# Two-layer attention trunk in split fp32: later score slots, token-tile stores for the turned q, k and gate, and a different final norm and store

## The chip, the cores and the metric

The kernel runs on one core of a Trainium2 chip. The metric is device time in microseconds (us) from launch to end, the median of several runs. The engines are named as in the profile: PE is TensorE (PEld its weight loads), DVE is VectorE, ACT is ScalarE, POOL is GpSimd and SP is SyncE, which here only issues DMAs. A letter q behind an engine's name (SPq, POOLq) stands for what it issues.

## The reference, cut to what matters

256 tokens of width 2048 go through two layers. Each layer is norm, one wide input projection, attention, a gate, one output projection and a residual add; a last norm closes.

```python
def _layer_c(x, norm_g, w_in, w_out, pos):
    h = jnp.matmul(_rmsnorm(x, norm_g).astype(x.dtype), w_in).astype(jnp.float32)
    cq, ck, cv, z = jnp.split(h, [C_WIDTH, 2 * C_WIDTH, 3 * C_WIDTH], axis=-1)
    yc = _moba_attention(_rope(_heads(cq, C_HEADS), pos), _rope(_heads(ck, C_HEADS), pos), _heads(cv, C_HEADS))
    y = _merge(yc) * jax.nn.silu(z)
    return x + jnp.matmul(y.astype(x.dtype), w_out)

def reference(x, ...):
    h = x
    for i in range(DEPTH):
        ...
    return _rmsnorm(h, final_norm).astype(x.dtype)
```

Layer 1 has 16 heads of 128; with 256 tokens its block attention is plain causal attention. Layer 0 has the same shape with two kinds of heads: eight heads whose three dilated windows are combined by their softmax denominators (which is one softmax with a count mask), and four differential heads (a softmax minus a learned multiple of a second one, times a value of width 256, then a norm).

## The kernel before, in words

**The projections.** Each layer is a row of 20 chunks of 512 output columns: four groups g of q, k, z (the gate) and v (g = 0 runs v, q, k, z), then four chunks `o` of the output projection. A chunk has 16 slots, one for each 128 rows of the contraction. In a slot PE runs `mm3` for each of two token tiles (128 tokens): three matmuls (high times high, high times low, low times high) give fp32 accuracy out of two rounded parts. So a slot is six matmuls of 512 columns, and the program has 40 chunks. The weights arrive as `raw` tiles of 1 MB (four slots, three buffers, issued by SP, L96) and are split for two slots at a time: ACT writes the high part `wh` (L122), then DVE the low part `wl` (L123). Split m serves slots 2m and 2m + 1 of the whole program. There are four buffers for each part, so ACT can write `wh` m only when PE is done with split m - 4.

**Between the projections.** `at(slot, f, ...)` puts a function behind the matmuls of a slot, and the loop over chunks calls what is due. For a finished q or k chunk, `nxt` is the first slot after it:

- `evac_rope` (L262) scales and rotates one token tile on DVE (L270 to L273, tiles `rt`), and `turn` (L233) transposes blocks of 32 by 32 within it (L235, tile `bz`). Tile 0 is due at `nxt`, tile 1 at `nxt + 2`.
- `place` (L238) follows tile 1: POOL stores both turned tiles to DRAM in one DMA of 512 KB (L243, tensor `dt`) and loads them back with eight DMAs of 64 KB (L247, four for each token tile), which finishes the transpose.
- `split_rope` (L278), at `nxt + 13`, splits the loaded tile into `kh`, `kl` (or `qh`, `ql`) on ACT and DVE (L285, L286), a token tile at a time for k.
- `attn_s` or `diff_s`, from `nxt + 14`, do the scores `ps_s` (L317 reads the raw tile `k`, then `mm3` the split ones) and the softmax. `attn_t` sends the probabilities `p` through DRAM in the same way (L356, L360), `attn_h` splits them (L369), and `attn_o` or `diff_o` with `diff_y` multiply by v and gate with the turned z (tile `u`).

These slots are due times. A scheduler puts each engine's instructions into one fixed list, and may draw something forward or push it back by where it thinks the data will be. Each engine then works through its list in order and waits at the first instruction whose input is missing. `order` rows below are taken from these lists.

**The end.** `last_chunk` (L456) runs token tile 0 as one piece of 512 columns and token tile 1 as two of 256. After each piece DVE adds the residual (L484), ACT squares and sums (L486), DVE adds to the mean (L491), POOL raises it to the power -0.5 (L493), DVE and ACT scale four pieces of 512 columns (L499, L501), and SP stores each (L502). At the start PE runs `WARM` matmuls on a constant (L137) before the first weights are split.

## Time and profile before

| | |
|---|---|
| median of 3 runs | 1003.44 us (997.42 to 1008.15) |
| the profiled execution, its time | 999.49 us |
| its span, first to last instruction | 997.7 us |
| mean granted TensorE clock | 0.971 |
| PE busy | 942.4 us (94%) |
| DVE busy | 643.0 us (64%) |
| ACT busy | 474.5 us (48%) |
| POOL busy | 200.5 us (20%) |
| HBM read and written | 192.23 MB and 20.19 MB, 213 GB/s over the span |

A busy PE is PE with a matmul in flight; at a lower granted clock the same matmul is busy for longer, so that busy time alone does not tell of a loss there. The rows in the prediction come from four kinds of views: the page (busy shares, costliest groups), the list of who waited for whom (engine, operation, line, what it waited for: us in total, times, longest), the timeline (start, duration, engine, line, operation, with the idle time before it and what ended that in brackets) and a table by stretches (length, busy time of each engine with the number of instructions, granted clock, DMA share, GB/s).

### The profile page before, as it was taken

To read this page: it belongs to the slowest core of one execution; us is meant where nothing else is said; L and a number is where in the kernel's file an instruction comes from. 1 tells how busy PE (TensorE), PEld (TensorE's weight loads), DVE (VectorE), ACT (ScalarE), POOL (GpSimd) and SP (SyncE) were. 2 spreads that over 40 slices of the span, in tenths; PEclk is the share of its full clock that TensorE was granted. 3 is DMA by queue.
4 is the path that set the end of the run, shared out by engine and by line. 5 is a ranking of instruction groups with operands and counts; after the bars stand their busy time and mean duration, and the time that the engine had idled before them with its cause. 6 is when DMAs were issued, how large, how long until landed. Compare 5 with 4: busy or idle time off the path is not lost. (4 is left out here: it accounts for less than half of the span.)

```text
span 997.7 us, 11928 instructions
## 1 busy us (share of the span) xinstructions
PE 942.4 (94%) x4276; PEld 778.8 (78%) x4276; DVE 643.0 (64%) x999; ACT 474.5 (48%) x711; POOL 200.5 (20%) x368
## 2 busy tenths in 40 slices
PE   8999997999799988999999999979996999799996
PEld 7887886888688867888888878868885888587886
DVE  6666875756566666665555768747664766575572
ACT  7534643553355335554554454535442644264451
POOL 0021441321113110300000125215011421132000
PEclk9999999999989998999999999989997999899999
DMA  9786776566645664655555668667665756676542
GB/s 329 259 320 232 242 241 212 198 210 244 214 161 210 213 232 137 220 196 174 187 193 185 237 212 266 219 199 234 212 209 180 245 198 211 211 241 227 187 169 84
DMA packets 42827, 213.21 MB, mean 214 GB/s; under 512 B 9040, under 2 KB 9808, under 8 KB 22672
## 3 DMA queue, kind: packets, MB, share of 16 engines
q1 hardware_dynamic: 27504, 175.21, 50.1%
q0 software_dynamic: 14976, 36.20, 11.4%
q10 hardware_dynamic: 288, 1.05, 0.3%
q8 instruction: 33, 0.54, 0.2%
q14 instruction: 26, 0.21, 0.1%
HBM read 192.23 MB, written 20.19 MB: 213 GB/s over the span
## 5 line engine op out<-in xcount | busy, mean ns | idle before, releaser
L312 PE MATMUL acc<-wh,x 128*128 128x512 f32 x2048 | 655.1, 397 | 1.6 <-ACT wh L119 1.6
L123 DVE TENSOR_TENSOR wl<-raw,wh 128x1024 fp32r<-128x1024 f32 x314 | 382.7, 1220 | 206.1 <-ACT wh L122 205.3
L122 ACT ACTIVATE wh<-raw 128x1024 fp32r<-128x1024 f32 x314 | 332.0, 1059 | 359.8 <-PE acc L312 322.2
L312 PEld LDWEIGHTS acc<-wh,x 128*128 128x128 f32 x2048 | 390.7, 191 | 81.9 <-ACT wh L119 1.8
L312 PE MATMUL acc<-wl,x 128*128 128x512 f32 x1024 | 405.1, 396 | 0.2 <-DVE wl L120 0.2
L312 PEld LDWEIGHTS acc<-wl,x 128*128 128x128 f32 x1024 | 196.0, 191 | 39.8 <-DVE wl L120 0.5
L312 PE MATMUL acc<-wh,yh 128*128 128x512 f32 x224 | 88.3, 394 | 0.0
L312 PE MATMUL acc<-wl,yh 128*128 128x512 f32 x224 | 87.4, 390 | 0.0
L312 PE MATMUL acc<-wh,yl 128*128 128x512 f32 x224 | 87.3, 390 | 0.0
L243 POOL DMA_DIRECT2D dt<-bz x24 | 13.6, 568 | 305.6 <-DVE bz L235 302.1
L360 POOL DMA_DIRECT2D p<-d x112 | 61.2, 554 | 56.8 <-DMA d<-bt 29.5
L317 PE MATMUL ps_s<-k,q 128*128 128x128 f32 x64 | 14.7, 315 | 41.8 <-DMA k<-dt 41.6
L317 PEld LDWEIGHTS ps_s<-k,q 128*128 128x128 f32 x64 | 12.8, 214 | 47.0 <-issue 29.8
L312 PEld LDWEIGHTS acc<-wh,yl 128*128 128x128 f32 x224 | 42.0, 188 | 9.1 <-DVE yl L389 0.3
L312 PEld LDWEIGHTS acc<-wl,yh 128*128 128x128 f32 x224 | 42.1, 188 | 8.4
L312 PEld LDWEIGHTS acc<-wh,yh 128*128 128x128 f32 x224 | 42.1, 188 | 8.2
L247 POOL DMA_DIRECT2D q<-dt x64 | 34.7, 550 | 39.2 <-ACT wh L122 19.7
L247 POOL DMA_DIRECT2D k<-dt x64 | 34.7, 549 | 32.6 <-DMA dt<-bz 19.6
L356 POOL DMA_DIRECT2D d<-bt x28 | 15.7, 561 | 124.3 <-DVE st L328 85.6
L247 POOL DMA_DIRECT2D u<-dt x64 | 34.7, 549 | 19.0 <-DMA p<-d 13.2
L286 DVE TENSOR_TENSOR kl<-k,kh 128x512 fp32r<-128x512 f32 x16 | 11.0, 688 | 39.1 <-ACT kh L285 39.1
L285 ACT ACTIVATE kh<-k 128x512 fp32r<-128x512 f32 x16 | 10.0, 624 | 44.3 <-DMA k<-dt 44.2
(122 smaller groups left out, 663.8 us busy)
## 6 DMA issues: line engine op xcount, KB each, us to landing
raw<-in_w SPq DMA_DIRECT2D x124, 1024.0 KB, 5.2
raw<-in_o SPq DMA_DIRECT2D x32, 1024.0 KB, 4.8
dt<-bz POOLq DMA_DIRECT2D x24, 512.0 KB, 4.2
d<-bt POOLq DMA_DIRECT2D x28, 192.0 KB, 4.3
p<-d POOLq DMA_DIRECT2D x112, 48.0 KB, 4.7
q<-dt POOLq DMA_DIRECT2D x64, 64.0 KB, 3.6
k<-dt POOLq DMA_DIRECT2D x64, 64.0 KB, 6.2
u<-dt POOLq DMA_DIRECT2D x64, 64.0 KB, 4.6
```

Of the source, the lines that this page charges most:

```text
L122: nc.scalar.activation(ht, r, AF.Copy)
L123: nc.vector.tensor_sub(lt, r, ht.bitcast(F32))
L243: nc.gpsimd.dma_start(d, bt.rearrange("p c t h j -> p c (t h j)"))
L247: nc.gpsimd.dma_start(t[32 * c:32 * c + 32, tt].rearrange("p a h j -> p a (h j)"), dv[c, tt])
L285: nc.scalar.activation(a, v, AF.Copy)
L286: nc.vector.tensor_sub(b, v, a.bitcast(F32))
L312: nc.tensor.matmul(out_, l, r, start=start and i == 0, stop=stop and i == 2)
L317: nc.tensor.matmul(ps[:, 0:P], q[:, h * P:(h + 1) * P], k[:, 0, :, h], start=True, stop=True)
L356: nc.gpsimd.dma_start(d, bt.rearrange("p c b j -> p c (b j)"))
L360: nc.gpsimd.dma_start(pt[32 * c:32 * c + 32], dv[c])
```

## The change

- `turn` now does the whole way for one token tile: its own `bz` (two buffers) and its own `dt` (256 KB, four buffers), stored as soon as that tile is turned. After tile 1 the eight loads are written as before, those of tile 0 from the first tensor and those of tile 1 from the second. `place` is gone.
- Tile 1 is due at `nxt + 1` (was `nxt + 2`).
- `split_rope` is due at `nxt + 18` (was 13). The first scores are due at `nxt + 22`, in the last group of a layer (g = 3, `late`) at `nxt + 20` (was 14). The slots of `attn_t`, `attn_h`, `attn_o`, `diff_o`, `diff_y` follow; for the heads of `attn_s` the distance from the last `attn_t` to its `attn_h` stays at 12 slots, and is 10 in the last group.
- `last_chunk`: the sum of squares is one DVE instruction with an accumulator (`tensor_tensor_reduce`) that starts from the mean so far; the last 256 columns are scaled and multiplied by the norm's weights in one instruction; the pieces are 256 and 512 columns wide, DVE's are stored by SP and ACT's by ACT itself, and token tile 1 has six pieces (was four).
- `WARM` is 13 (was 10).

```diff
-WARM = 10
+WARM = 13
...
-    def turn(src, bt, tt):
-        nc.vector.transpose(bt[:, :, tt].rearrange("p c h j -> p h c j"),
-                            src.rearrange("p (h c j) -> p h c j", h=4, c=4))
-    def place(bt, name):
-        t = work.tile([P, 2, 4, 4, 32], F32, tag=name, name=name)
-        d = dram.tile([P, 4, S], F32, tag="dt", name="dt")
-        nc.gpsimd.dma_start(d, bt.rearrange("p c t h j -> p c (t h j)"))
-        dv = d.rearrange("(a i) c (t x) -> c t i a x", a=4, t=2)
-        for tt in range(2):
-            for c in range(4):
-                nc.gpsimd.dma_start(t[32 * c:32 * c + 32, tt].rearrange("p a h j -> p a (h j)"), dv[c, tt])
-        return t
+    def turn(src, box, name):
+        tt = len(box)
+        bt = work.tile([P, 4, 4, 32], F32, tag="bz", name="bz", bufs=2)
+        nc.vector.transpose(bt.rearrange("p c h j -> p h c j"), src.rearrange("p (h c j) -> p h c j", h=4, c=4))
+        d = dram.tile([P, 4, P], F32, tag="dt", name="dt", bufs=4)
+        nc.gpsimd.dma_start(d, bt.rearrange("p c h j -> p c (h j)"))
+        box[tt] = d.rearrange("(a i) c x -> c i a x", a=4)
+        if tt == 1:
+            box["t"] = t = work.tile([P, 2, 4, 4, 32], F32, tag=name, name=name)
+            for i in range(2):
+                for c in range(4):
+                    nc.gpsimd.dma_start(t[32 * c:32 * c + 32, i].rearrange("p a h j -> p a (h j)"), box[i][c])
...
-                nc.scalar.activation(j, x, AF.Square, accum_out=fs[:, tt, i:i + 1])
...
+                mean = e5[:, tt, 3 + i:4 + i]
+                nc.vector.tensor_tensor_reduce(out=j, in0=x, in1=x, scale=1.0 / D, scalar=part, op0=ALU.mult,
+                                               op1=ALU.add, accum_out=mean)
+                part = mean
+                if i + 1 == len(widths):
+                    nc.gpsimd.tensor_tensor(rf, mean, half, op=ALU.pow)
+                if tt == 0 or i == 0:
+                    nc.vector.tensor_mul(x, x, gf[1][:, CW + at_col:CW + at_col + w])
...
+            pieces = ((0, 256), (256, 768), (768, 1280), *last), ((1280, 1536), (1536, mid))
...
+                    (nc.sync, nc.scalar)[e].dma_start(out[tt * P:(tt + 1) * P, c[0]:c[1]], x)
...
-                    at(nxt + 2 * tt, evac_rope, ps, kind, (Q, K)[kind == "k"], layer, g, tt, box)
+                    at(nxt + tt, evac_rope, ps, kind, (Q, K)[kind == "k"], layer, g, tt, box)
             if kind != "z":
-                at(nxt + 13, split_rope, kind, (Q, K)[kind == "k"], layer, g, box)
+                at(nxt + 18, split_rope, kind, (Q, K)[kind == "k"], layer, g, box)
...
+            late = g == 3
+            first = nxt + (20 if late else 22)
...
-                    at(nxt + 14 + 3 * h, attn_s, layer, g, h, md if layer == 0 else mc, box)
-                    at(nxt + 17 + 3 * h, attn_t, box)
-                    at(nxt + 32 + 2 * h, attn_h, box)
-                    at(nxt + 34 + 2 * h, attn_o, layer, g, h, box)
+                    at(first + 3 * h, attn_s, layer, g, h, md if layer == 0 else mc, box)
+                    at(first + 3 + 3 * h, attn_t, box)
+                    at(first + (13 if late else 15) + 3 * h, attn_h, box)
+                    at(first + (15 if late else 17) + 3 * h, attn_o, layer, g, h, box)
```

The diff moves a few numbers; what they do to the lists stands in the following rows, all of the last group of layer 1. There k's chunk ends at slot 544 (`nxt`), `acc544` is the gate's chunk and `acc560` that of v, `x0` to `x15` are the 16 slots of a chunk, and split m serves slots 2m and 2m + 1, so that the number behind `wh` tells the slot. Line numbers of the change differ by a few from those of before (L243 is L242, L247 is L248, L285 is L279, L122 is L123).

PE, the place of the first score matmul of the group, before:

```order
L312 MATMUL acc544_6717<-wh279_6812,x14_115 128x512
L317 MATMUL ps_s_6880<-k_6761,q_6593 128x128
L312 MATMUL acc544_6717<-wh279_6812,x15_116 128x512
L312 MATMUL acc544_6717<-wl279_6813,x15_116 128x512
L312 MATMUL acc544_6717<-wh279_6812,x15_116 128x512 x2
```

and with the change:

```order
L306 MATMUL acc560_6952<-wh282_6934,x4_108 128x512
L311 MATMUL ps_s_7030<-k_6818,q_6652 128x128
L306 MATMUL ps_s_7030<-kh_7008,qh_6839 128x256
L306 MATMUL ps_s_7030<-kl_7009,qh_6839 128x256
L306 MATMUL ps_s_7030<-kh_7008,ql_6840 128x256
L306 MATMUL acc560_6952<-wh282_6934,x5_109 128x512
```

The first score moves from the gate's slot 15, which is `nxt` + 15, to v's slot 5, `nxt` + 21 (in the other groups to `nxt` + 23), and is now followed at once by its other three matmuls.

ACT, the place of the copies that split k, before:

```order
L122 ACTIVATE wh281_6846<-raw140_6798 128x1024
L122 ACTIVATE wh282_6868<-raw141_6832 128x1024
L285 ACTIVATE kh_6862<-k_6761 128x4x128
L122 ACTIVATE wh283_6901<-raw141_6832 128x1024
L285 ACTIVATE kh_6862<-k_6761 128x4x128
```

and with the change:

```order
L123 ACTIVATE wh279_6884<-raw139_6831 128x1024
L279 ACTIVATE kh_7008<-k_6818 128x4x128
L123 ACTIVATE wh280_6900<-raw140_6870 128x1024
L123 ACTIVATE wh281_6918<-raw140_6870 128x1024
L279 ACTIVATE kh_7008<-k_6818 128x4x128
L123 ACTIVATE wh282_6934<-raw141_6904 128x1024
```

Although `split_rope` is due five slots later, its copy of token tile 0 now stands three weight splits earlier, ahead of split 280 (needed at slot 560, `nxt` + 16), and that of tile 1 two earlier, ahead of split 282 (`nxt` + 20). All eight groups have this distance.

POOL, the store and the loads of k (`dt` and `k`) and what follows, before:

```order
L243 DMA dt_6762<-bz_6728 128x1024
L247 DMA k_6761<-dt_6762 32x4x128 x8
L356 DMA d_6926<-bt_6924 128x384
L243 DMA dt_6965<-bz_6911 128x1024
L360 DMA p_6886<-d_6926 32x4x96 x4
```

and with the change:

```order
L242 DMA dt_6800<-bz_6798 128x512
L248 DMA k_6818<-dt_6800 32x4x128 x4
L242 DMA dt_6816<-bz_6814 128x512
L248 DMA k_6818<-dt_6816 32x4x128 x4
L242 DMA dt_6970<-bz_6968 128x512
L248 DMA u_6987<-dt_6970 32x4x128
```

The four loads of tile 0 stand ahead of the store of tile 1, though the code writes them behind it; the store of tile 1 waits in this list until they are issued.

## The prediction

> **What bounds the kernel now.** I first read the page's busy shares and the list of waits. The columns of the latter are engine, operation, line, what it waited for, and the time in total, the number of waits and the longest.

> ```profile
> PE 942.4 (94%) x4276; PEld 778.8 (78%) x4276; DVE 643.0 (64%) x999; ACT 474.5 (48%) x711; POOL 200.5 (20%) x368
> PE ps_s L317 <- DMA k<-dt: 41.6, 7, 7.9
> PE ps_s L312 <- ACT kh L285: 1.8, 2, 1.6
> ```

> PE is the bound, and nearly all its idle time behind the start is one wait: the first score matmul of a group waits for the k that comes back from DRAM, seven times of eight, for 41.6 us. The timeline shows where, and how fast PE runs otherwise.

> ```profile
> 75.56 0.39 PE L312 MATMUL acc<-wl,x 128*128 128x512 f32 x1
> 76.24 0.39 PE L312 MATMUL acc<-wl,x 128*128 128x512 f32 x1
> ...
> 174.25 0.77 PE L317 MATMUL ps_s<-k,q 128*128 128x128 f32 x2 [5.91 <-DMA k<-dt]
> ...
> 868.92 0.76 PE L317 MATMUL ps_s<-k,q 128*128 128x128 f32 x2 [6.69 <-DMA k<-dt]
> ```

> From one `wl` matmul to the next there are 0.68 us and three matmuls, so a slot of six is 1.36 us. Two of the seven waits stand in brackets. Such a wait has a second price, seen when the stretch of 10 us that begins with its end is asked for. The columns are the stretch, its length, busy time of PE, PEld, DVE, ACT and POOL, granted clock, DMA share and GB/s.

> ```profile
> 96.95:106.95 10.00, 9.75 (x46) 7.92 (x47) 7.32 (x20) 7.96 (x17) 0.00 (x0) 1.00 0.50 175
> 174.25:184.25 10.00, 10.00 (x41) 8.29 (x42) 6.01 (x17) 6.59 (x16) 0.00 (x0) 0.80 0.33 113
> 274.88:284.88 10.00, 10.00 (x37) 8.25 (x38) 5.15 (x15) 5.46 (x13) 0.00 (x0) 0.71 0.30 106
> 378.05:388.05 10.00, 10.00 (x39) 8.28 (x40) 5.50 (x15) 5.97 (x13) 0.00 (x0) 0.75 0.31 107
> 664.34:674.34 10.00, 10.00 (x38) 8.26 (x39) 5.37 (x16) 5.94 (x13) 0.00 (x0) 0.73 0.32 114
> 767.36:777.36 10.00, 10.00 (x39) 8.29 (x40) 5.64 (x17) 6.23 (x14) 0.00 (x0) 0.76 0.30 105
> 868.92:878.92 10.00, 10.00 (x37) 8.26 (x38) 5.26 (x16) 6.01 (x12) 0.00 (x0) 0.72 0.30 105
> ```

> PE is busy all through, but at a mean clock of 0.71 to 0.80 after six of the waits: it lost 2.0 + 2.9 + 2.5 + 2.7 + 2.4 + 2.8 = 15.3 us of work. The seventh, the shortest, left the clock at 1.00. So the late k costs 41.6 + 15.3 = 56.9 us of the span of 997.7.

> **The change, part by part.** *Later scores.* The scores go from `nxt` + 15 to `nxt` + 23 (+ 21 in the last group of a layer), which is 8 x 1.36 = 10.9 us later (8.2). The longest wait was 7.9 us (in the list of waits), so on this count alone the 41.6 us and the clock loss go. What is late next? The copies that split k, since ACT's list now has them ahead of weight splits (the rows of the change). Their deadline, counted from the end of k's chunk: `wh` and `wl` of slot 16 are needed at 16 x 1.36 = 21.8 us, and kh, wh and wl come one after the other:

> ```profile
> L123 DVE TENSOR_TENSOR wl<-raw,wh 128x1024 fp32r<-128x1024 f32 x314 | 382.7, 1220 | 206.1 <-ACT wh L122 205.3
> L122 ACT ACTIVATE wh<-raw 128x1024 fp32r<-128x1024 f32 x314 | 332.0, 1059 | 359.8 <-PE acc L312 322.2
> L285 ACT ACTIVATE kh<-k 128x512 fp32r<-128x512 f32 x16 | 10.0, 624 | 44.3 <-DMA k<-dt 44.2
> ```

> 0.62 + 1.06 + 1.22 and 0.2 for the hand-overs are 3.1 us. So token tile 0 may land at 18.7 us, and tile 1 (slot 20, 27.2 us) at 24.1 us, before PE waits. Queued behind the waiting copy on ACT are the next `wh`, then the gate's evacuation; behind those `wl` on DVE, and PE behind both. How long k takes, from the second group of layer 0 (first q, then k, then the store, the loads and the landing) and from the first group, where it came quickest:

> ```profile
> 123.30 0.75 DVE L270 SCALAR_TENSOR_TENSOR rt<-acc,rn,cosN 128x512 f32<-128x512 f32 x1 [0.35 <-PE acc L312]
> 128.25 0.70 DVE L235 STREAM_TRANSPOSE bz<-rt 128x512 f32<-128x512 f32 x1
> 133.16 0.70 DVE L235 STREAM_TRANSPOSE bz<-rt 128x512 f32<-128x512 f32 x1
> 147.98 0.75 DVE L270 SCALAR_TENSOR_TENSOR rt<-acc,rn,cosN 128x512 f32<-128x512 f32 x1 [0.71 <-PE acc L312]
> 151.69 0.63 ACT L285 ACTIVATE qh<-q 128x512 fp32r<-128x512 f32 x1 [2.59 <-DMA q<-dt]
> 155.23 0.71 DVE L235 STREAM_TRANSPOSE bz<-rt 128x512 f32<-128x512 f32 x1
> 160.29 0.70 DVE L235 STREAM_TRANSPOSE bz<-rt 128x512 f32<-128x512 f32 x1
> 161.29 0.56 POOL L243 DMA_DIRECT2D dt<-bz  x1 [15.87 <-DVE bz L235]
> 165.39 4.33 POOL L247 DMA_DIRECT2D k<-dt  x8 [3.55 <-ACT wh L122]
> 174.04 0.63 ACT L285 ACTIVATE kh<-k 128x512 fp32r<-128x512 f32 x1 [5.96 <-DMA k<-dt]
> ...
> 91.57 4.34 POOL L247 DMA_DIRECT2D k<-dt  x8 [3.29 <-DMA dt<-bz]
> 96.67 0.63 ACT L285 ACTIVATE kh<-k 128x512 fp32r<-128x512 f32 x1 [1.72 <-DMA k<-dt]
> ```

> From the end of k's chunk (147.98) the turn of tile 0 starts at 7.25 us, since DVE stood behind q's split (151.69), while for q it starts at 4.95. Tile 1's starts at 12.31 (q: 9.86), the store at 13.31, the loads 4.10 later, and k is there 8.65 after the first load (5.10 in the first group), at 26.06.

> *Stores by token tile.* q gains the same way and lands before k's rotation, so I put the turn of k's tile 0 between the two rows, at 6.3, and its store at 7.3. The half store I give the whole one's 4.10: loads at 11.4. Four loads move half of what eight do, so I take a landing between 5.10 and 8.65, 6.5: tile 0 at 17.9, 0.8 us early. POOL issues four loads in 4.33 / 2 = 2.17 us and takes tile 1's store only then (13.6; its turn ends by about 12), so its loads start at 17.7 and land at 24.2, 0.1 late. With 5.10 nothing waits; with 8.65 tile 0 is 1.35 and tile 1 2.25 us late, 2.25 a group. I take 0.8 a group for the scatter, **6.5 us** for eight groups (0 to 18); no such wait is long enough for the clock. The 24 extra stores cost POOL 24 x 0.56 = 13.4 us at 20% busy, under PE's cover unless they delay loads, which the sum above counts.

> [...]

> *Scores' end.* The heads' p follow later, and the output projection does not move. In the last group the fourth head has from `nxt` + 30 to + 45, 20.4 us.

> ```profile
> d<-bt POOLq DMA_DIRECT2D x28, 192.0 KB, 4.3
> p<-d POOLq DMA_DIRECT2D x112, 48.0 KB, 4.7
> ```

> Store and landing 4.3, the issue of four loads 2.2, their landing 4.7 and the split 1.0 are 12.2, which leaves 8.2 us for softmax and turn. Those are some ten instructions of 128 to 384 columns, each shorter than the 0.62 to 0.75 us that 512 columns take above; 6 us is my estimate from that. So this is hidden by 2 us, and I cost it at nothing. The 1.8 us of waits for kh may stay or go: **-0.9** (0 to 1.8).

> *Start.* Three more warming matmuls fill PE's gap before the first weights:

> ```profile
> 1.06 3.95 PE L137 MATMUL pw<-ones 128*128 128x128 f32 x20 [1.06 <-DVE fs L463]
> 6.62 0.49 PE L312 MATMUL acc<-wh,x 128*128 128x512 f32 x1 [1.61 <-ACT wh L119]
> 7.60:11.00 3.40, 3.40 (x9) 2.65 (x9) 1.53 (x4) 1.89 (x4) 0.00 (x0) 0.51 0.99 330
> ```

> Six records of 3.95 / 20 = 0.2 us end at 6.2, ahead of 6.62, so they delay nothing. PE then ran 3.4 us at 0.51, a loss of 1.7, which a shorter gap may or may not spare: **-1.0** (0 to 1.7).

> [...]

> *End.* The sum of squares loses its trip to ACT:

> ```profile
> 989.84 0.42 DVE L484 TENSOR_TENSOR x_sb<-last,x_sb 128x256 f32<-128x256 f32 x1 [4.14 <-PE last L475]
> 990.35 0.42 ACT L486 ACTIVATE junk_l<-x_sb 128x256 f32<-128x256 f32 x1 [5.25 <-DVE x_sb L484]
> 991.19 0.66 POOL L493 TENSOR_TENSOR fs<-fs,half 128x1 f32<-128x1 f32 x1 [10.08 <-DVE fs L491]
> L322 DVE CUSTOM_DVE_ANT_0 p<-ps_s,mc x48: 249/338/426, 282.9 to 887.2; 128x128 f32<-128x128 f32 x24, 128x256 f32<-128x256 f32 x24
> 981.89 12.32 SPq L502 DMA_DIRECT2D out<-x_sb  x8
> ```

> From the add's end (990.26) to POOL are 0.93 us; one accumulating instruction of 256 columns takes 0.43 (L322's longest) and about 0.1 to be read, so 0.4 is saved. The first store can start 0.2 earlier on top with half the columns, and the last one is half as large. The store queue ran until 981.89 + 12.32 = 994.21 and the span ends at 997.7, so landing dominates: **-0.8** (0 to 1.3).

> *Sum*, against this execution: 997.7 - 56.9 + 6.5 - 0.9 - 1.0 - 0.8 = 944.6, and 1.8 for what lies around the span (999.49 - 997.7): **946 us**. The median of the runs is 4.0 us above the profiled execution. I don't add that, since runs can differ by how long the clock stays down after a wait, and those waits go.

> **The rivals.** *The wait moves to ACT.* Token tiles land as slowly as the rows of before allow: turn at 7.25, store 8.25, loads 12.35, landing 21.0 (2.3 late); tile 1's store 14.5, loads 18.6, landing 27.25 (3.15 late). 8 x 3.15 = 25 us instead of 6.5: **965**. For it speak the six slow landings, against it that half as much is loaded at once and that q is no longer late.

> *Slower.* The half store brings nothing, and tile 0 lands when k does now, at 26.06, while its copy has been drawn three splits forward. Then PE waits 26.06 - 18.7 = 7.4 us for the split of slot 16, loses some 2.5 to the clock (as after the six waits), eight times: 79 us instead of 6.5, **1019**. It decides from where a group costs (999.5 - 946 + 6.5) / 8 = 7.5 us with the clock, a wait of 5.0, that is a landing at 23.7. Against it: tile 0's turn ends 5 us before tile 1's in the rows, and its store no longer waits for that.

> *The probabilities come late.* In the last group the loads of two heads stand together in POOL's list (eight loads, 4.4 us), which can eat the cover. With 2 us for each of the four heads in layer 1's last group, **954**.

> *Another engine becomes the bound.* DVE would be busy 643 of 946, 68%; nothing speaks for it.

> **How the numbers follow.** Forecast 0.75, wait on ACT 0.16, late probabilities 0.04, slower 0.03, and 0.02 for no change. The forecast's own bounds are 997.7 - 56.9 - 1.8 - 1.7 - 1.3 + 1.8 = 938 and 997.7 - 56.9 + 18 + 1.8 = 961. Stretching the top to the first rival gives 938 to 965, with about 0.8 inside. A measurement of this kernel can tell about 1% from no change: faster 0.95, same 0.02, slower 0.03.

> **What would show it.** Right: PE's waits for k are gone from the list, the clock row has no stretch near 0.7 in the middle, ACT's waits for k (44.2 us now) stay or grow, and stores of `dt` come in pairs. The first score runs at once behind the matmuls before it. Wrong: PE waiting on `wh` or `wl` by more than 18 us in total, or on p; a granted clock of a half behind such a wait; a span above 963.

## The result, and the profile after

The changed kernel takes 958.62 us (median of four runs, 949.69 to 960.44). The kernel before took 1000.43 us (median of four, 997.42 to 1008.15) on the same chip. The ratio is 0.9553, 95% interval 0.9467 to 0.9639. Ratios leave out runs more than 1.5% above the fastest of the same kernel: none here, but in the two series of the experiments two and four of the seven runs of the kernel before and one of the kernel with the stores alone, so that the second series' ratios rest on three of them and its kernels are best compared with each other. The forecast was 946 us, with a range of 938 to 965: the time lies inside, 12.6 us above the forecast. The profiled execution took 960.44 us, with a span of 958.7 and a mean granted clock of 0.991 (before: 997.7 and 0.971).

The busy row and the list of PE's waits come first, since the forecast was a sum over such waits.

```profile
PE 931.4 (97%) x4282; PEld 773.0 (81%) x4282; DVE 646.2 (67%) x1002; ACT 467.5 (49%) x705; POOL 214.8 (22%) x392
```

```profile
PE po L306 <- ACT th L363: 10.6, 3, 5.5
PE po L306 <- DVE y L381: 2.7, 2, 1.3
PE ps_yt L416 <- DVE yb L407: 2.4, 1, 2.4
PE acc L306 <- DVE wl L124: 2.0, 5, 0.7
...
PE pdo L306 <- ACT th L363: 0.2, 1, 0.2
```

The waits for k are gone, all seven, and those for `kh` too. In the list of all waits, ACT now waits for k where PE did: 58.2 us in 16 waits. PE hardly feels it: 2.0 us for `wl`, of which 0.67 at the start. What stands at the top is new: PE waits for `th`, the high part of the probabilities. With the waits behind it in the chain of the heads (`y`, `yb`) that is 10.6 + 0.2 + 2.7 + 2.4 = 15.9 us. The timeline has these waits in three places: the first group of layer 0 (heads 1 and 3), the last group of layer 0, and the first group of layer 1 (1.33 us for `y` and, with head 3, 4.54 for `th`).

```profile
139.09 0.35 PE L306 MATMUL po<-th,vh 128*128 128x256 f32 x1 [1.33 <-DVE y L381]
...
155.32 0.58 PE L306 MATMUL po<-th,vh 128*128 128x256 f32 x1 [5.55 <-ACT th L363]
...
410.17 0.74 PE L416 MATMUL ps_yt<-ident,yb 128*128 128x128 f32 x4 [2.38 <-DVE yb L407]
...
629.46 0.39 PE L306 MATMUL po<-th,vh 128*128 128x256 f32 x1 [4.54 <-ACT th L363]
```

And the stretches of 10 us behind the three longer ones, where the granted clock is the number ahead of the last two:

```profile
155.32:165.32 10.00, 10.00 (x39) 8.41 (x40) 8.66 (x14) 3.75 (x5) 3.15 (x6) 0.82 0.51 157
410.17:420.17 10.00, 10.00 (x39) 7.95 (x40) 6.45 (x10) 4.99 (x9) 0.00 (x0) 0.83 0.36 111
629.46:639.46 10.00, 10.00 (x39) 8.31 (x40) 8.74 (x14) 3.74 (x5) 3.30 (x6) 0.83 0.53 156
```

They lost 1.8 + 1.7 + 1.7 = 5.2 us to the clock; behind the waits of 1.33 us it was at 1.00. So late probabilities cost 15.9 + 5.2 = 21.1 us, in a part of the program that I had costed at nothing.

**Why they are late** stands in POOL's rows for the first group. The first row stores head 3's probabilities, and the last one loads them back.

```profile
134.42 0.56 POOL L350 DMA_DIRECT2D d<-bt  x1
136.81 0.57 POOL L248 DMA_DIRECT2D q<-dt  x1 [1.83 <-ACT th L363]
138.93 0.55 POOL L242 DMA_DIRECT2D dt<-bz  x1 [1.56 <-DVE bz L240]
139.47 1.66 POOL L248 DMA_DIRECT2D q<-dt  x3
143.53 2.17 POOL L248 DMA_DIRECT2D q<-dt  x4 [2.40 <-DMA dt<-bz]
145.69 2.18 POOL L354 DMA_DIRECT2D p<-d  x4
```

Between the store of `d` and the loads of `p` stand all eight loads of the next group's q and its second store, with waits of 1.83, 1.56 and 2.40 us: 145.69 - 134.42 = 11.27 us from store to loads. PE wanted `th` at 155.32 - 5.55 = 149.77. ACT's list adds its part, since the same q is split ahead of `th`:

```profile
151.31 0.63 ACT L279 ACTIVATE qh<-q 128x512 fp32r<-128x512 f32 x1 [5.99 <-DMA q<-dt]
...
154.87 0.40 ACT L363 ACTIVATE th<-p 128x256 fp32r<-128x256 f32 x1
```

The trace also tells when the four loads of `p` landed: 5.6 to 6.5 us after their issue, the last of them (issued at 147.3) at 152.9. That is 3.1 us after PE wanted `th`; the other 2.4 us of the wait of 5.55 lie behind the landing, 2.0 of them in ACT's list.

**k itself** comes when the forecast wanted it, on the mean of the eight groups. Here is the second group of layer 0, for which the forecast had its rows. The first two rows are q's split and the start of k's rotation on DVE (tile 0), the others are the copies of k's tiles 0 and 1, which waited for the landing:

```profile
152.62 0.69 DVE L280 TENSOR_TENSOR ql<-q,qh 128x512 fp32r<-128x512 f32 x1
153.22 0.74 DVE L266 SCALAR_TENSOR_TENSOR rt<-acc,rn,cosN 128x512 f32<-128x512 f32 x1
...
169.88 0.63 ACT L279 ACTIVATE kh<-k 128x512 fp32r<-128x512 f32 x1 [2.24 <-DMA k<-dt]
...
177.37 0.63 ACT L279 ACTIVATE kh<-k 128x512 fp32r<-128x512 f32 x1 [4.33 <-DMA k<-dt]
```

The last of the 96 matmuls of k's chunk ends at 147.51. So the rotation does not follow its chunk at once, as it does in the kernel before: it starts 5.7 us later, since DVE's list has the split of q ahead of it, and q is late. Counted from the end of the chunk, as the forecast counts, tile 0 is there after 169.88 - 147.51 = 22.4 us and tile 1 after 29.9 (forecast: 17.9 and 24.2). PE does not wait for it there: in that time it stands 5.55 us for `th` and loses 1.8 to the clock, so that it reaches the splits behind k's copies later as well. In the last group of layer 1 it is 14.5 and 21.2 us. Over all eight groups tile 0 takes 14.5 to 22.4 us (mean 18.4) and tile 1 20.0 to 29.9 (mean 24.0). The rotation starts 0.7 to 5.9 us behind the chunk (mean 3.0); in the kernel before it was 0.04 in each group.

At the **end**, the add of the last columns and the power on POOL, the rows that answer to 989.84 and 991.19 of before:

```profile
951.11 0.42 DVE L477 TENSOR_TENSOR x_sb<-last,x_sb 128x256 f32<-128x256 f32 x1 [4.34 <-PE last L468]
...
952.14 0.55 POOL L484 TENSOR_TENSOR e<-e,half 128x1 f32<-128x1 f32 x1 [9.90 <-DVE e L480]
```

From the add's start to POOL's power it is 1.03 us (before 991.19 - 989.84 = 1.35), and to the end of the span 958.7 - 951.1 = 7.6 (before 7.9).

### The profile page after: what moved, and what is told of

It is laid out like the page before. It is cut to its first block, busy times and chain, and to the rows that moved or that the text cites. A ratio compares the mean times of both kernels' runs of the same rounds, so it can differ in the third digit from the quotient of the medians.

```text
span 958.7 us, 11998 instructions
## 1 busy us (share of the span) xinstructions
PE 931.4 (97%) x4282; PEld 773.0 (81%) x4282; DVE 646.2 (67%) x1002; ACT 467.5 (49%) x705; POOL 214.8 (22%) x392
## 3 DMA queue, kind: packets, MB, share of 16 engines
q0 software_dynamic: 15360, 36.20, 11.4%
## 5 line engine op out<-in xcount | busy, mean ns | idle before, releaser
L306 PE MATMUL acc<-wh,x 128*128 128x512 f32 x2048 | 645.8, 392 | 0.0
L306 PEld LDWEIGHTS acc<-wh,x 128*128 128x128 f32 x2048 | 385.7, 188 | 79.0 <-ACT wh L120 0.5
L123 ACT ACTIVATE wh<-raw 128x1024 fp32r<-128x1024 f32 x314 | 328.5, 1055 | 224.3 <-PE acc L306 202.6
L306 PE MATMUL acc<-wl,x 128*128 128x512 f32 x1024 | 400.5, 391 | 2.5 <-DVE wl L124 2.0
L306 PEld LDWEIGHTS acc<-wl,x 128*128 128x128 f32 x1024 | 193.0, 189 | 43.3 <-DVE wl L124 4.6
L242 POOL DMA_DIRECT2D dt<-bz x48 | 27.3, 569 | 264.4 <-DVE bz L240 264.0
L248 POOL DMA_DIRECT2D k<-dt x64 | 34.9, 552 | 66.0 <-DMA dt<-bz 40.2
L248 POOL DMA_DIRECT2D u<-dt x64 | 35.0, 553 | 57.0 <-DMA dt<-bz 57.0
L248 POOL DMA_DIRECT2D q<-dt x64 | 35.0, 554 | 55.3 <-DMA dt<-bz 46.2
L320 ACT ACTIVATE p<-p,st 128x128 f32<-128x128 f32 x64 | 28.5, 447 | 33.1 <-DVE st L316 33.1
L280 DVE TENSOR_TENSOR kl<-k,kh 128x512 fp32r<-128x512 f32 x16 | 11.1, 693 | 43.5 <-ACT kh L279 43.5
L279 ACT ACTIVATE kh<-k 128x512 fp32r<-128x512 f32 x16 | 10.1, 632 | 58.2 <-DMA k<-dt 58.2
L363 ACT ACTIVATE th<-p 128x256 fp32r<-128x256 f32 (+1 forms) x28 | 12.0, 428 | 53.8 <-DMA p<-d 51.5
L364 DVE TENSOR_TENSOR tl<-p,th 128x256 fp32r<-128x256 f32 (+1 forms) x28 | 12.3, 439 | 26.8 <-ACT th L363 26.8
## 6 DMA issues: line engine op xcount, KB each, us to landing
d<-bt POOLq DMA_DIRECT2D x28, 192.0 KB, 3.4
```

What stands on the lines that cost most here:

```text
L123: nc.scalar.activation(ht, r, AF.Copy)
L242: nc.gpsimd.dma_start(d, bt.rearrange("p c h j -> p c (h j)"))
L248: nc.gpsimd.dma_start(t[32 * c:32 * c + 32, i].rearrange("p a h j -> p a (h j)"), box[i][c])
L279: nc.scalar.activation(a, v, AF.Copy)
L280: nc.vector.tensor_sub(b, v, a.bitcast(F32))
L306: nc.tensor.matmul(out_, l, r, start=start and i == 0, stop=stop and i == 2)
```

## The experiments

The theory was: the k waits went because of both the later slots and the stores by token tile, and what lies between 946 and 958.6 is the probabilities, held up in POOL's list by the next group's q. Eight kernels, one of them the change itself, were timed in two series of four, each series on one chip beside the kernel before. All ratios are to the kernel before, with 95% intervals. Spans are those of each kernel's profiled execution.

| kernel | median us (lowest to highest) | ratio | span |
|---|---|---|---|
| first series: slots alone | 971.14 (970.31 to 976.78) | 0.9708 (0.9621 to 0.9795) | 969.8 |
| stores alone | 971.97 (968.92 to 986.63) | 0.9692 (0.9607 to 0.9777) | 972.7 |
| q of group 1 four slots later | 943.89 (942.48 to 948.27) | 0.9429 (0.9361 to 0.9498) | 940.7 |
| group 0 with the last group's slots | 952.00 (950.53 to 953.24) | 0.9502 (0.9438 to 0.9566) | 950.0 |
| second series: the change again | 957.33 (952.30 to 961.42) | 0.9578 (0.9494 to 0.9663) | 950.5 |
| q loads of group 1 from SP | 947.29 (942.20 to 951.54) | 0.9478 (0.9400 to 0.9556) | 949.8 |
| q of group 1 six slots later | 941.48 (940.73 to 951.41) | 0.9455 (0.9341 to 0.9569) | 939.0 |
| the change with the old start and end | 962.29 (956.30 to 970.43) | 0.9636 (0.9530 to 0.9741) | 962.4 |

### The slots alone

The kernel before, with the later slots of the change (of the score, softmax and output slots only one line is shown). Tile 1 of a chunk stays due at `nxt + 2`:

```diff
-                at(nxt + 13, split_rope, ...)
+                at(nxt + 18, split_rope, ...)
...
+            first = nxt + (20 if late else 22)
...
-                    at(nxt + 14 + 3 * h, attn_s, ...)
+                    at(first + 3 * h, attn_s, ...)
...
```

> The later slots alone: whole stores and eight loads at a time as before, and the old start and end. My theory: the slots take the scores' 41.6 us and the clock's 15.3 away, but a k that lands as before, some 26 us behind its chunk, meets the copy kh, which stands ahead of the split of slot 19 (due at 18.7 + 3 x 1.36 = 22.8). PE then waits for wl some 2 to 3.3 us in each of eight groups, 16 to 26 in all, with up to 2 us of half clock behind each: 960 to 985, 968 as the middle. POOL's list has all probabilities ahead of the next q, so PE's wait for th in the first group of each layer is gone. Rival (the slots carry the whole gain, the stores none): PE's waits for wl stay under 5 us in all, and without the late probabilities the time is below the change's 958.6, 940 to 950.

Measured: 971.14 us, near the middle of my range, and for another reason than I gave. PE's waits of that kernel:

```profile
PE po L312 <- DVE y L387: 6.2, 6, 2.4
PE po L312 <- ACT th L369: 4.1, 2, 2.8
PE pdo L312 <- ACT th L369: 3.8, 1, 3.8
PE acc L312 <- DVE wl L123: 3.5, 6, 0.8
...
PE po L312 <- DVE tl L370: 1.8, 2, 1.4
PE acc L312 <- ACT wh L122: 1.6, 3, 1.2
```

For weights it is 3.5 + 1.6 = 5.1 us, not 16 to 26. My deadline was wrong: a split serves two slots, so a copy that stands three splits later has 6 x 1.36 = 8.2 us more and not 4.1, and is due at 18.7 + 8.2 = 26.9. Tile 0 of k came 20.3 to 29.8 us behind its chunk (mean 27.1), just about then. The rest, 6.2 + 4.1 + 3.8 + 1.8 = 15.9 us, is late probabilities again, here in six of the eight groups, though no q stands ahead of them. POOL's rows for the second group of layer 0 show what does: all eight loads of the gate (behind its whole store), and the stores of two heads ahead of the loads of either.

```profile
185.32 4.42 POOL L247 DMA_DIRECT2D u<-dt  x8 [2.92 <-DMA dt<-bz]
189.73 0.56 POOL L356 DMA_DIRECT2D d<-bt  x1
...
196.81 4.37 POOL L360 DMA_DIRECT2D p<-d  x8 [5.45 <-DMA d<-bt]
```

From head 0's store to its loads it is 7.1 us. The slots alone take PE's k waits away (2.2 us for `kh` and 0.4 for `kl` are left, in one group). Late probabilities are not what sets this kernel apart from the change, since there too they cost PE 15.9 us. By the lists of waits, what the stores by token tile add is an earlier k: 5.1 - 2.0 = 3.1 us less for weights and 2.6 less for `kh` and `kl`. That is 5.7 of the 11.1 us between the two spans (969.8 and 958.7); the rest is not assigned.

### The stores alone

The change, with the slots, the start and the end of before (again one line of the score, softmax and output slots; the last chunk of before is not shown). Tile 1 of a chunk is due at `nxt + 1`, as in the change, so that this slot goes with the stores:

```diff
-WARM = 13
+WARM = 10
...
-                at(nxt + 18, split_rope, ...)
+                at(nxt + 13, split_rope, ...)
...
-            first = nxt + (20 if late else 22)
...
-                    at(first + 3 * h, attn_s, ...)
+                    at(nxt + 14 + 3 * h, attn_s, ...)
...
```

> The stores by token tile alone, with the slots, start and end of before. My theory: tile 1 of k lands at about 24.2 us behind its chunk and is split by 25.5, while the first score, at nxt + 15, wants it at 20.8: PE waits some 4.7 us for kh or kl in each group, with some 2 us of half clock behind it, 8 x 6.7 = 54 instead of 56.9: 985 to 998. Rival (the stores carry the gain): the waits of the scores fall below 1 us a group, 945 to 960.

Measured: 971.97 us, below both bounds of my theory and above the rival's. PE waits for `kh` 15.7 us in six waits and for `kl` 1.4, where I expected 8 x 4.7 = 38. The DMA rows say in part why; their columns are the count, KB each and the median us from issue to landing. The kernel before:

```profile
k<-dt POOLq DMA_DIRECT2D x64, 64.0 KB, 6.2
```

the slots alone:

```profile
k<-dt POOLq DMA_DIRECT2D x64, 64.0 KB, 6.1
```

the stores alone:

```profile
k<-dt POOLq DMA_DIRECT2D x64, 64.0 KB, 4.0
```

and the change:

```profile
k<-dt POOLq DMA_DIRECT2D x64, 64.0 KB, 3.7
```

In both kernels with eight loads in a row a load of k lands 6.1 or 6.2 us after its issue; in both with two times four it lands after 3.7 or 4.0. That it is the number in a row is not shown by this: the moment of issue moved too, and q's loads went the other way (3.6 us before, 4.6 in the change). The store itself gains little by being halved: in the same view the whole store's median is 4.2 us in the kernel before and 3.8 with the slots alone, the half store's 4.1 in the change and 3.5 here. From the end of k's chunk, tile 1 is there after 19.2 to 26.5 us (mean 21.9), so here the stores by token tile bring k some 2 us sooner than the 24.2 that I gave them. Still, the score at `nxt` + 15 is too early in six groups, the first of them by 6.12 us. Neither part alone reaches the change: each stays some 13 us behind it, and all runs of both (from 968.92 us) lie above the slowest of the change (961.42). That both are needed is shown by this; how the 13 us divide is only read from the lists.

### The second group's q four slots later

```diff
-                    at(nxt + tt, evac_rope, ...)
+                    at(nxt + tt + (4 if kind == "q" and g == 1 else 0), evac_rope, ...)
```

> The change, with one slot number moved: the second group's q is taken out of PSUM four slots later, so that POOL's list has the fourth head's p loads of each layer's first group ahead of the next group's q store and loads. Score and output slots stay. My theory (the loads stood behind q's in POOL's list, and th behind qh in ACT's): PE's waits of 5.55 and 4.54 us for th, the 1.33 us for y ahead of them and their 3.5 us of half clock go, about 16 us, leaving 958.6 - 16 = 943, 940 to 948; the wait of 2.4 us for yb in layer 0's last group stays. Rival (the p loads land late because the weight loads share the DMA engines, whatever stands ahead of them): landing stays 6 us behind the issue and PE's wait for th stays above 3 us in each layer, 953 to 960.

Measured: 943.89 us, where 943 was expected. Its ratio's interval still touches that of the change (0.9467 to 0.9639), but its slowest run (948.27) is below the fastest of the change in either series (949.69). POOL's rows for the same place now have the loads of `p` right behind their store's landing, and q's behind those:

```profile
133.72 0.56 POOL L350 DMA_DIRECT2D d<-bt  x1 [0.20 <-issue]
...
138.48 2.20 POOL L354 DMA_DIRECT2D p<-d  x4 [1.75 <-DMA d<-bt]
```

From store to loads it is 138.48 - 133.72 = 4.8 us instead of 11.27, and PE has no wait for `th` left in the list. Two points were not as I wrote: the wait for `y` in the first group grew from 1.33 to 2.44 us, and the one for `yb` in the last group of layer 0 was not there in this execution. So the match with 943 is in part luck. Of the theory's own terms 11.0 us came: 10.1 for `th` and 3.5 of half clock went, while the waits for `y` grew by 0.9 in all and the longer of them brought 1.7 of half clock (0.83 in the 10 us behind it). The `yb` wait, which I had expected to stay, was another 2.4 + 1.7 us.

### The first group with the slots of the last

```diff
-            late = g == 3
+            late = g in (0, 3)
```

> The change, with the first group of each layer given the slots of the last one: scores two slots earlier, outputs four slots earlier (13 instead of 15 behind a head's scores). POOL's list then has all p loads of that group ahead of the next group's q store. My theory (list order): the waits for th and y in the first groups and their half clock go, 14 to 16 us, 942 to 948, though the outputs have 2.7 us less room than in the change. Rival (landing on busy DMA engines, or the room that the slots leave): with less room PE waits longer for th than now, over 5 us in each layer's first group, 958 to 968.

Measured: 952.00 us, 4 us above the theory's range and 6 below the rival's. PE's waits in the two first groups fell from 12.8 us (1.33 + 5.55 + 1.33 + 4.54) to 7.2, not to nothing:

```profile
PE po L306 <- DVE y L381: 5.1, 2, 3.3
PE po L306 <- ACT th L363: 2.3, 2, 2.1
```

POOL, head 3's store and the start of head 2's loads in the first group of layer 0:

```profile
131.35 0.56 POOL L350 DMA_DIRECT2D d<-bt  x1 [4.79 <-DVE bt L348]
131.90 0.57 POOL L354 DMA_DIRECT2D p<-d  x1
```

q is out of the way, but head 2's loads now stand behind head 3's store, which waits 4.79 us for DVE. Moving one thing out of the list's way put another into it.

### The change again, and q's loads from SP's queue

The change was timed once more, to stand beside three variants.

> The change itself, to have it beside the variants in one series. Any theory: its ratio to the kernel before falls in the 0.947 to 0.964 of the first series, and the same waits for th stand in the first group of each layer.

Measured: 957.33 us and a ratio of 0.9578, as expected. Its profiled execution took 952.30 us, with a span of 950.5:

```profile
PE po L306 <- ACT th L363: 9.5, 2, 5.7
```

The two waits for `th` are there (5.68 and 3.81 us), and the one for `yb` is not. In all PE waits 14.1 us here and 19.4 in the other execution of the same program; the wait for `yb` is 2.4 of these 5.3 us, and what sets the two executions apart was not shown.

The next kernel leaves q's slots alone and takes only its eight loads out of POOL's list:

```diff
-        turn(t1, box, name)
+        turn(t1, box, name, nc.sync if name == "q" and g == 1 else None)
...
-                    nc.gpsimd.dma_start(t[32 * c:32 * c + 32, i]...
+                    (eng or nc.gpsimd).dma_start(t[32 * c:32 * c + 32, i]...
```

> The change, with the second group's eight q loads of each layer issued from SP's queue instead of POOL's; the slots, the rotation of q on DVE and the stores stay. My theory (the fourth head's p loads stood behind q's loads and the wait of 2.40 us among them): the p loads start some 4 to 6 us earlier than in the change, PE's waits of 5.55 and 4.54 us for th go, and 10 us with 3.5 us of half clock are gained: about 945, 941 to 950. The waits for y (1.33 us each) stay, since DVE's list does not change. Rival (DMA engines busy with weights, whatever the list): the p loads land 6 us behind their issue and later than PE wants them, a wait over 3 us for th stays in each layer, 953 to 960. A second rival: SP's next weight load, now queued behind q's, comes late and PE waits for weights.

Measured: 947.29 us, with all four runs below the lowest of the change in this series. POOL:

```profile
136.16 0.56 POOL L350 DMA_DIRECT2D d<-bt  x1
...
141.20 2.20 POOL L354 DMA_DIRECT2D p<-d  x4
```

From store to loads it is 5.0 us. ACT waited for `p` and took it up at 146.75, 5.5 us behind the first issue: the issue and the landing take that long on their own, which is the rival's half of the truth. But the 11.27 - 5.04 = 6.2 us that POOL's list had cost are gone, and with them PE's wait for `th` in both first groups. The landing was shorter too: 3.8 to 4.9 us a load here and 3.1 to 4.1 with q four slots later, against 5.6 to 6.5 in the change, where eight loads of q are issued right ahead. In the last groups of the two layers waits of 1.1 and 1.5 us for `th` and one of 2.4 for `yb` stand in this execution. The wait of 1.33 us for `y` in the first group stayed, since DVE's list is as in the change; in layer 1 it was not seen. PE's waits for `wl` rose from 2.0 to 5.1 us, none above 1.2: the second rival, weights that come late behind q's loads, was not seen to cost more than that.

In both variants the scheduler also put `th` ahead of `qh` on ACT. How much of the 5.55 us was ACT's list and how much POOL's is therefore only read from rows: ACT reached `th` 3.56 us after it started `qh` at 151.31 (the copy, `yh`, another copy and a split), 2.0 of them after `p` had landed, and that `qh` itself waited for the q loads.

### Six slots instead of four

```diff
-                    at(nxt + tt, evac_rope, ...)
+                    at(nxt + tt + (6 if kind == "q" and g == 1 else 0), evac_rope, ...)
```

> As the variant with the second group's q four slots later, but six slots later. My theory: there PE's wait of 2.44 us for y is DVE's, which has q's rotation ahead of y; two slots more move the rotation behind it, and that wait and its 1.7 us of half clock go: 4 us less than the four-slot variant, about 940. Rival (y is late because its own p landed late): the wait stays, 943 to 945. PE is then busy for all but some 10 us, so nothing below 937 is to be had this way.

Measured: 941.48 us, the best of all, its median 15.9 us below that of the change in the same series. But it is not told apart from the variant with four slots, and the waits for `y` that I meant to remove are still there:

```profile
PE po L306 <- DVE y L381: 4.1, 2, 2.4
```

They were 3.5 us with four slots (2.44 and 1.07; here 1.63 and 2.42). Moving q's rotation by two more slots did not free `y`; what holds it up stays open. The 1.7 us of half clock did go: in the 10 us behind each of the two waits the granted clock was 1.00, where it was 0.83 behind the 2.44.

### The old start and end

The change with the start and the last chunk of before:

```diff
-WARM = 13
+WARM = 10
...
-                nc.vector.tensor_tensor_reduce(out=j, in0=x, in1=x, scale=1.0 / D, scalar=part, ...)
+                nc.scalar.activation(j, x, AF.Square, accum_out=fs[:, tt, i:i + 1])
...
-                    (nc.sync, nc.scalar)[e].dma_start(...)
+                nc.sync.dma_start(out[tt * P:(tt + 1) * P, n * CW:(n + 1) * CW], x)
```

> The change without its start and its end: ten warming matmuls and the last chunk of before, with the new slots and stores. By the traces of before and after, the start gains 0.23 us (first q rotation at 53.09 and 52.86) and the end 0.27 (7.86 and 7.59 us from the last add to the end of the span), so this kernel is 0.5 us slower than the change, by rows; the forecast had 1.8. Both are below what the times can tell: the rows of start and end decide. Rival (start and end carry a visible part): over 3 us slower than the change of the same series.

Measured: 962.29 us, 5 above the change, with ranges that overlap (956.30 to 970.43 and 952.30 to 961.42). The rows have to tell:

```profile
52.79 0.75 DVE L266 SCALAR_TENSOR_TENSOR rt<-acc,rn,cosN 128x512 f32<-128x512 f32 x1 [0.40 <-PE acc L306]
...
839.30 0.79 PE L306 MATMUL acc<-wh,x 128*128 128x512 f32 x1 [2.50 <-ACT wh L123]
...
954.49 0.42 DVE L478 TENSOR_TENSOR x_sb<-last,x_sb 128x256 f32<-128x256 f32 x1 [4.14 <-PE last L469]
```

The end takes 962.4 - 954.5 = 7.9 us, as before, so the new end is worth 0.3. The first rotation of q is at 52.79 us, not later than with thirteen warming matmuls (52.86 and 53.07 in the two executions of the change, 52.62 to 52.92 in the four variants of it with thirteen). Most of the 5 us is elsewhere in this execution: tile 1 of the last k landed late and PE waited 2.50 us for the split behind it, with the clock at 0.68 for the 10 us after. That is the rival "the wait moves to ACT", seen once.

## Why the prediction was right, and where it was not

**What bounds the kernel: right.** PE's waits for k and the half clock behind them were the 56.9 us, and all of it went. Busy time of PE fell from 942.4 to 931.4 us with six more small matmuls, as the stretches at half clock became fewer (the mean granted clock is 0.971 before and 0.991 with the change).

**"Later scores" and the copies' deadline: right.** What came next was, as forecast, ACT waiting for k, and PE for `wl` where a copy is late.

**"Stores by token tile": the times right on the mean, the price too high.** From the end of k's chunk 17.9 and 24.2 us were forecast, and 18.4 and 24.0 came on the mean. From the first load of tile 0 to its copy it is 4.3 to 8.8 us, 6.5 on the mean, as I took it. (The quickest landing of the kernel before was not the 5.10 us that I started from but 3.9, in the first group of layer 1.) What I had wrong beside it is that "q gains the same way and lands before k's rotation": in four of the eight groups q's copy started 0.7 to 3.8 us after the end of k's chunk, and k's rotation waited behind it. The price that I put on the scatter, 0.8 us a group and 6.5 in all, did not come: 2.0 us at most were measured, 0.46 the longest such wait behind the start. The two groups in which k came latest (tile 1 after 29.9 and 26.4 us) are those in which PE itself stood for `th`, so that there the lateness was covered by another one. That "no such wait is long enough for the clock" the kernel before shows for 1.73 us, the shortest of its waits for k (1.00 in the 10 us behind it); for waits up to the 2.25 us of the upper end it was my estimate, and in the change 2.38 us, for `yb`, had 0.83 behind them. I gave the half store the time of the whole one; the medians from issue to landing are 4.1 and 3.5 us for the half and 4.2 and 3.8 for the whole.

**"Scores' end ... hidden by 2 us, and I cost it at nothing": wrong**, and it is the step that makes the 12.6 us, and more. The prediction had named it as a sign of being wrong: PE waits on p, with a stretch of half clock behind. I worked out the cover for the last group alone, since its slots are the tightest. In the first group of each layer the slots leave 2.7 us more, but there POOL's list has the next group's q between a head's store and its loads. The list of the changed kernel could have shown that; I counted the DMAs that the moved step issues and not those that it is moved past. It cost 21.1 us in the profiled execution. The rival "the probabilities come late" had the wait, with a chance of 0.04, a price of 2 us a head, the wrong group and another reason (the loads of two heads together in POOL's list, which is what the kernel with the slots alone shows). Taking q's loads out of the way gave 943.89, 947.29 and 941.48 us, around the forecast's 946.

**Start: the size wrong.** The half clock of the kernel before came back in two of three other executions with ten warming matmuls. The views give 1.00 there, because the record of the clock begins only at 10.6 us (slots alone) and 10.0 (stores alone), but PE's pace shows it. With the slots alone:

```profile
8.61 0.63 PE L312 MATMUL acc<-wl,x 128*128 128x512 f32 x1
...
9.89 0.63 PE L312 MATMUL acc<-wl,x 128*128 128x512 f32 x1
```

From one `wl` matmul to the next it is 1.28 us, where it is 0.68 at full clock. With thirteen warming matmuls PE was at full pace from 8 us on, wherever it did not wait, in all six executions (in the change 0.68 to 0.70 us from one `wl` matmul to the next). So the three matmuls may well have spared the half clock; ten executions do not show it for certain. It brought little all the same: at full pace PE met waits for the split weights instead (0.67 us at 14.16 in the change), and the first rotation of q starts at 53.04 us on the mean with ten and at 52.82 with thirteen, 0.2 us sooner where I gave 1.0.

**End: right in sign**, 0.3 instead of 0.8. From the end of SP's row of last stores to the end of the span it is 3.5 us in the kernel before (994.2 to 997.7) and 3.7 in the change (955.0 to 958.7), so this stretch did not shrink with the last store.

**The sum** by what was measured: 997.7 - 56.9 (k) - 1.8 (`kh`) + 21.1 (probabilities) + 1.3 (`wl` behind the start) - 0.2 - 0.3 = 960.9, against a span of 958.7. The 2.2 us that are left are not assigned; 0.8 of them are two small waits of before, for `th` and `v`. That the time lies inside the range is in part luck. With the late probabilities alone the forecast's own sum would be 944.6 + 21.1 = 965.7 us of span, and 967.5 us of time, above the range; 5.2 us too much for k's lateness and the smaller terms brought it back. And the top of the range had been set by another rival, the wait on ACT.

**"Those waits go", so the runs would agree better: wrong.** The runs of the change spread over 10.7 us, as before. The two profiled executions differ by 8.2 us of span, of which some 7 are waits (19.4 - 14.1 = 5.3) and the half clock behind the one for `yb` (1.7). With q six slots later three of four runs lie within 1 us and the fourth is 10 above.

## What to carry to other kernels

When a step is moved later, read what it now stands behind on every engine's list, the queue that issues its DMAs above all. Here a store and its load on one queue left a gap, and what was put between them was added to the round trip with its waits: 11.27 us from store to loads with eight loads and a store of q between them, 4.8 with q four slots later and 5.0 with its loads on SP's queue. Do that for each distinct group, not only for the one with the tightest slots. And treat a stall in one profiled execution as one draw: the wait of 2.38 us for `yb` was not there in the second execution of the same program, and the half clock behind a wait was there at 2.44 us and not at 2.42.

## What the runs showed of the hardware

```profile
152.17:159.00 6.83, 3.68 (x11) 3.21 (x12) 5.42 (x10) 3.21 (x6) 0.56 (x1) 0.50 0.24 74
411.58:415.00 3.42, 3.42 (x10) 2.53 (x9) 2.42 (x5) 1.80 (x3) 0.00 (x0) 0.50 0.72 232
```

and this one to the wait of 6.12 us (up to 102.27) in the kernel with the stores alone:

```profile
98.73:108.97 10.24, 6.56 (x16) 5.11 (x17) 5.23 (x13) 4.83 (x9) 0.56 (x1) 0.50 0.36 129
```

They last 6.8, 3.4 and 10.2 us. The change has one more, of 3.4 us, behind its wait of 4.54. In the kernel before, three k waits (5.60, 5.91 and 6.13 us) have one of 6.8 and three (6.69, 7.67 and 7.88) one of 10.2; these are those of the waits of 6.13 and 6.69:

```profile
273.80:280.63 6.83, 5.75 (x15) 4.62 (x16) 1.99 (x3) 2.98 (x5) 0.00 (x0) 0.50 0.02 6
864.31:874.55 10.24, 5.63 (x14) 4.55 (x15) 1.87 (x3) 2.87 (x5) 1.09 (x2) 0.50 0.25 79
```

So 6.13 us went with the shorter one there, and 6.12 in the kernel with the stores alone with the longer one. A part of such a stretch can lie inside the wait, where it costs nothing: behind the 5.55 us there were 159.0 - 155.3 = 3.7 us of it left, a loss of 1.8, and behind the 6.12 us 6.7. A wait of 2.77 us in the kernel with the slots alone was followed by none:

```profile
885.44:895.44 10.00, 9.93 (x45) 7.59 (x46) 5.84 (x9) 4.45 (x8) 0.00 (x0) 1.00 0.36 137
```

Behind the start, two shorter waits had half clock after them: 2.38 us (in the change) and 2.44 us (q four slots later), each with 0.83 in the 10 us behind it. Others had 1.00 there: 1.33 us (in the change), 1.73 us (k in the kernel before) and 2.42 us (q six slots later). What decides it, these runs do not show.
